# One 512-column matmul for both input parts in the four side-by-side output tiles of a mixer

## The chip, the cores and the metric

The kernel runs on one core of a Trainium2 chip. The metric is the device time of one execution in microseconds (us), as the median of several. The engines that matter are TensorE (PE in the profile; PEld is its weight loading), ScalarE (ACT), VectorE (DVE) and the DMA queues that SyncE (SP) issues. Each engine works through its own list of instructions; they wait for each other on semaphores. The schedule of TensorE, ACT and DVE is written by hand in this kernel: their instructions run in the order in which the program issues them.

## The reference

An encoder trunk of 4 layers for 256 tokens of width 1024. Each layer is a SwiGLU feed-forward block, a mixer and a second feed-forward block, each between two RMS norms and added to the stream x:

```python
for i in range(DEPTH):
    g = norm_g[i]
    x = x + 0.5 * rms_norm(swiglu(rms_norm(x, g[0]), ff1_w_in[i], ff1_w_out[i]), g[1])
    h = rms_norm(x, g[2])
    kind, j = i % N_MIXERS, i // N_MIXERS
    if kind == 0:
        m = mixer_a(h, a_w_qkv[j], a_rel_bias[j], a_w_o[j])
    elif kind == 1:
        m = mixer_b(h, b_w_in[j], b_ln_g[j], b_ln_b[j], b_w_s[j], b_b_s[j], b_w_o[j])
    else:
        m = mixer_c(h, c_w_qkv[j], c_lambda[j], c_subln_g[j], c_w_o[j], lambda_init)
    x = x + rms_norm(m, g[3])
    x = x + 0.5 * rms_norm(swiglu(rms_norm(x, g[4]), ff2_w_in[i], ff2_w_out[i]), g[5])
```

Mixer A (layers 0 and 3) is chunked attention with a relative bias, mixer B (layer 1) a gated MLP that mixes positions, mixer C (layer 2) differential attention. Each ends in the product `o @ w_o` with a 1024 x 1024 matrix, followed by the norm with gain g[3]. That output product is what the change touches.

## The kernel before

**Layout.** Activations stand transposed: the channel on the 128 partitions, the token along the row. 1024 channels are 8 blocks k of 128 input channels, or 8 tiles d of 128 output channels, each of 256 tokens (S).

**Precision.** A product in full fp32 precision is made of fp32r matmuls on split operands. A value is split into a high part (rounded to fp32r) and a low part (the rest); of the four products, high x high, high x low and low x high are summed. For an input x the parts are called h and l and lie side by side as `x[:, 0, :]` and `x[:, 1, :]`, 256 columns each. For a weight they are `wh` and `wl`.

**Weights.** `Stream` (W in the code) loads them in slices, of which a piece of 128 x 1024 is half. A piece is split by a cast on ACT (L126, `w_hi`) and a subtraction on DVE (L129, `w_lo`). `W.pump` issues the next splits, `W.settle` issues the subtraction that is still pending, `W.done` gives a piece's slot free, and `W.hold` and `W.resume` stop and restart the splitting. There are 8 slots. A piece holds all 8 blocks k of one output tile of the mixer's output product.

**Two kinds of products.** `product` (L168) issues, for each k, three matmuls of 256 columns into one accumulator of 256 columns: wh x h, wh x l and wl x h. `product2` (L182) issues two per k: wh with h and l together as 512 columns, and wl with h as 256 columns. Its accumulator has 512 columns, of which the two halves have to be added at the end. In the down product of a feed-forward block `Branch.joined` does that: ACT copies the second half from PSUM (L363), DVE adds it to the first half into the tile `yg` (L364), and `tile_done` then works from `yg`.

**The end of a tile.** `Branch.tile_done` takes a finished tile, from PSUM or from `yg`. ACT squares it (L373, for the norm's sum over channels) and scales it with the gain into `yg` (L374). DVE adds the square to the sum (L384). After tiles 4 and 5 `Ahead.tile_done` splits tiles 0 to 3 of `yg` for the next block's first product (L407 on ACT, L408 on DVE). After the last tile, TensorE sums over the partitions with a column of ones (L243), first the sum of tiles 0 to 6 and then the square of tile 7. ACT takes the root (L251), DVE the reciprocal (L253), and TensorE spreads the result over the partitions (L258). DVE then forms the update of x (L473, L479), and the next feed-forward block begins (L507). Between those steps TensorE works off a list of matmuls of that next block which can be done with the old x and the unscaled `yg` (`Ahead`, L448, 24 matmuls), so many at each place.

**The output product.** `project_out` makes tiles 0 to 3 side by side, k by k, because its inputs come in k by k as the mixer ends, and tiles 4 to 7 one after the other by `product`. For the first four the order of steps is

```python
ORDER = (0,F) (1,F) (0,T) (2,F) (1,T) (3,F) (2,T) ... (7,F) (6,T) (7,T)     # (k, low)
```

A first step (F) of a k issues wh x h and wl x h for each of the four tiles; a low step (T) issues wh x l. Ahead of the first step of each k, `between(k)` issues what the mixer still has to do: transposes of probabilities (L763), their products with the values (L885, L886 in mixer A; L1102, L1104 in C), L986 in mixer B, the transposes L1132 in C, and the splits of the result into h and l on ACT and DVE. From k = 2 on, each low step also issues the split of one weight piece.

**PSUM.** `pair()` gives one of three buffers of two banks, a bank being 512 columns of fp32. The four tiles side by side take one bank each, so two buffers; each of tiles 4 to 7 takes a buffer of its own. `bank()` gives one of two single banks for transposes, sums and spreads.

Of the kernel before, what the change touches and what calls it, by code (L numbers as in the profile page):

```python
# [18 lines left out]
S = 256  # L19
DEPTH = 4  # L20
KD = D // P
# [35 lines left out]
def encoder_trunk_kernel(  # L57
# [14 lines left out]
    nc = tc.nc  # L72
# [91 lines left out]
    def product(o, wh, wl, x, ks, at, start, stop):  # L164

        for i, k in enumerate(ks):
            for m, (w_, low) in enumerate(((wh, 0), (wh, 1), (wl, 0))):
                nc.tensor.matmul(  # L168
                    o, w_[:, at + i, :], x(k)[:, low, :], start=(start and i == 0 and m == 0),
                    stop=(stop and k == ks[-1] and m == 2),  # L170
                )
# [16 lines left out]
    def pair():  # L188
        return pp.tile([P, 2, 512], F32, tag="pp", name="pp_t")
# [208 lines left out]
    class Ahead:  # L398
# [7 lines left out]
        def parts(self, dst, src, scale):  # L406
            nc.scalar.activation(dst[:, 0, :], src, AF.Copy, scale=scale)  # L407
            nc.vector.scalar_tensor_tensor(  # L408
                dst[:, 1, :], src, scale, dst[:, 0, :].bitcast(F32), op0=ALU.mult, op1=ALU.subtract
            )  # L410
# [82 lines left out]
    def blocks(piece):  # L493
        return [part.rearrange("p (k c) -> p k c", k=KD) for part in piece]
# [144 lines left out]
    def project_out(parts, l, between, ahead):  # L639

        br = Branch(g_sb[:, l, 3, :], None, ahead)
        ws = [blocks(W.peek(e)) for e in range(4)]
        os = [ps[:, e, 0:S] for ps in (pair(), pair()) for e in range(2)]
        for k, low in ORDER:
            if not low:
                between(k)
            x = parts(k)
            for (wh, wl), o in zip(ws, os):
                for part in (wh,) if low else (wh, wl):
                    nc.tensor.matmul(  # L650
                        o, part[:, k, :], x[:, int(low), :], start=(k == 0 and part is wh and not low),
                        stop=(k == KD - 1 and low), skip_group_check=True,
                    )
            if low and k >= PUMP:
                W.pump(1)
        W.settle()
        for d in range(4):
            br.tile_done(d, os[d])
        W.done(4, 1)
        for d in range(4, KD):  # L660
            o = pair()[:, 0, 0:S]
            wh, wl = blocks(W.peek())
            product(o, wh, wl, parts, range(KD), 0, True, True)
            if d == KD - 1:
                W.hold()
                W.done()
            br.tile_done(d, o)
            if d < KD - 1:
                W.done(1, 1)
        return br.finish()  # L670
# [159 lines left out]
    def mixer_a(l, i, update):  # L830
# [86 lines left out]

        late = attention(n, softmax, transposes, v_done, mix)
        return project_out(parts, l, between, ahead)

    def mixer_b(l, i, update):
# [95 lines left out]
        def between(k):  # L1017
# [3 lines left out]
            if k == 3:  # L1021
                split(3)
                nc.scalar.preload_act_table(AF.Sqrt)

        return project_out(lambda k: op[:, k], l, between, ahead)

    def mixer_c(l, i, update):
# [144 lines left out]
        ss = small.tile([P, 16], F32, tag="sso", name="sso", bufs=1)  # L1172
        late = attention(n, softmax, transposes, v_done, mix, prepare, lambda: split(0))
        return project_out(parts, l, between, ahead)

    mixers = (mixer_a, mixer_b, mixer_c)
# [87 lines left out]
```

## Time and profile before

| | us |
|---|---|
| median of 3 runs | 1946.46 (1946.42 to 1948.36) |
| profiled execution, device time | 1947.0 |
| profiled execution, span from first to last instruction | 1945.3 |
| TensorE busy | 1931.1 |
| DVE busy | 1378.4 |
| ACT busy | 1169.6 |

The granted clock of TensorE was 0.997 of full speed over the span. The profile comes from one execution. A group's line gives the line of the program, the engine and operation, the tile written and those read, the shape and count, then the busy time and the mean duration in ns, then the idle time of the engine ahead of these instructions and what ended it. In the chain of waits each row has a start, a length and the instructions merged into it, both times in us. In a timeline a row has a start, a length, the engine and line, and in brackets how long the engine stood idle before it and for what. In a table of windows a row has the stretch, its length, the busy time and count of each engine, the granted clock, the share of the DMA engines' time, and GB/s. The durations of matmuls overlap, since they are pipelined: the time from one start to the next is shorter than one duration.

### The profile page before, as it was taken

How to read it: one execution, taken by the hardware profiler on the slowest of the kernel's cores; microseconds unless marked ns; L12 is line 12 of the kernel's file. 1: busy time of each engine (PE TensorE's matmuls, PEld its weight loads, DVE VectorE, ACT ScalarE, POOL GpSimd, SP SyncE). 2: the span in 40 equal slices, each digit the busy share in tenths (PEclk: the TensorE clock that was granted, in tenths of full speed). 3: DMA queues.
4: the chain of work that ended last, by engine and by line, in shares of the span. 5: the costliest groups of instructions: out<-in, count | busy, mean ns of one | idle time of the engine just before them, and what ended most of it. 6: DMA issues, size and time to landing. Idle time of an engine off the chain costs nothing.

```text
span 1945.3 us, 30035 instructions
## 1 busy us (share of the span) xinstructions
PE 1931.1 (99%) x12402; PEld 1745.4 (90%) x12402; DVE 1378.4 (71%) x1883; ACT 1169.6 (60%) x1805; POOL 5.2 (0%) x19
## 2 busy tenths in 40 slices
PE   9999999999999999999999999999999999999998
PEld 8888999888988889888988899988898888999887
DVE  6775867866777577877677668786767766868763
ACT  6655657656655565756565565675656555656552
POOL 0000000000000000000000000000000000000000
PEclk9999999999999999999999999999999999999999
DMA  7555524655455543655455544255545554535551
GB/s 262 205 184 202 190 108 154 232 189 184 171 196 186 205 163 141 216 195 182 165 195 195 195 155 174 109 200 196 188 155 213 180 206 161 197 123 183 203 201 44
DMA packets 50393, 350.30 MB, mean 180 GB/s; under 512 B 5712, under 2 KB 5968, under 8 KB 9040
## 3 DMA queue, kind: packets, MB, share of 16 engines
q1 hardware_dynamic: 48096, 341.86, 49.0%
q10 hardware_dynamic: 2160, 6.52, 0.9%
q8 instruction: 97, 1.59, 0.3%
q14 instruction: 40, 0.33, 0.1%
HBM read 347.31 MB, written 1.05 MB: 179 GB/s over the span
## 4 chain that ended last, share of the span: by engine, by line
PE 98%; DVE 1%; ACT 0%; DMA 0%; ACTq 0%; issue 0%; SPq 0%; DVEq 0%
PE pp_t L182 68%; PE pp_t L526 8%; PE pp_t L168 7%; PE pp_t L507 4%; PE pp_t L691 3%; PE pp_t L650 2%; PE pp_t L731 1%; PE pst_t L763 1%; PE pst_t L243 1%; PE pp_t L448 1%; PE pst_t L258 1%; PE pst_t L448 1%; PE pp_t L885 0%; PE pp_t L446 0%; DVE upd L473 0%; DMA w_raw<-in_w 0%
## 5 line engine op out<-in xcount | busy, mean ns | idle before, releaser
L129 DVE TENSOR_TENSOR w_lo<-w_raw,w_hi 128x1024 fp32r<-128x1024 f32 (+1 forms) x649 | 776.4, 1218 | 69.6 <-ACT w_hi L126 69.6
L126 ACT CAST w_hi<-w_raw 128x1024 fp32r<-128x1024 f32 (+1 forms) x649 | 668.9, 1046 | 160.1 <-PE pp_t L182 130.7
L182 PE MATMUL pp_t<-xp,w_hi 128*128 128x512 f32 x2560 | 613.7, 391 | 0.0
L182 PEld LDWEIGHTS pp_t<-xp,w_hi 128*128 128x128 f32 x2560 | 469.7, 188 | 90.4
L182 PEld LDWEIGHTS pp_t<-xp,w_lo 128*128 128x128 f32 x2560 | 329.0, 191 | 12.5
L182 PE MATMUL pp_t<-xp,w_lo 128*128 128x256 f32 x2560 | 334.6, 283 | 0.0
L597 DVE TENSOR_TENSOR gu<-pp_t,share 128x512 f32<-128x512 f32 x160 | 110.7, 692 | 206.1 <-ACT share L596 206.1
L596 ACT COPY share<-pp_t 128x512 f32<-128x512 f32 x160 | 93.6, 585 | 150.5 <-PE pp_t L182 149.5
L182 PE MATMUL pp_t<-h,w_hi 128*128 128x512 f32 x672 | 169.0, 391 | 0.0
L182 PE MATMUL pp_t<-l,w_hi 128*128 128x512 f32 x560 | 142.6, 391 | 0.0
L182 PEld LDWEIGHTS pp_t<-h,w_hi 128*128 128x128 f32 x672 | 122.1, 189 | 22.6
L567 ACT ACTIVATE gs<-gs 128x512 f32<-128x512 f32 x88 | 55.7, 633 | 141.5 <-DVE gs L566 141.5
L526 PE MATMUL pp_t<-xp,w_hi 128*128 128x256 f32 x832 | 123.8, 288 | 1.6 <-ACT xp L319 0.8
L182 PEld LDWEIGHTS pp_t<-l,w_hi 128*128 128x128 f32 x560 | 102.5, 188 | 21.1 <-DVE l L576 1.6
L526 PEld LDWEIGHTS pp_t<-xp,w_hi 128*128 128x128 f32 x832 | 111.1, 193 | 3.7 <-ACT xp L319 1.0
L364 DVE TENSOR_TENSOR yg<-pp_t,share 128x256 f32<-128x256 f32 x56 | 23.8, 425 | 108.8 <-ACT share L363 108.8
L182 PEld LDWEIGHTS pp_t<-h,w_lo 128*128 128x128 f32 x672 | 91.1, 191 | 5.0
L182 PE MATMUL pp_t<-h,w_lo 128*128 128x256 f32 x672 | 95.1, 282 | 0.0
L182 PE MATMUL pp_t<-l,w_lo 128*128 128x256 f32 x560 | 80.6, 283 | 0.0
L319 ACT ACTIVATE xp<-xr,g_sb 128x256 fp32r<-128x256 f32 x96 | 44.8, 504 | 56.4 <-DVE xr L479 54.0
L182 PEld LDWEIGHTS pp_t<-l,w_lo 128*128 128x128 f32 x560 | 75.3, 191 | 2.9
L526 PE MATMUL pp_t<-xp,w_lo 128*128 128x256 f32 x416 | 73.8, 284 | 0.0
(196 smaller groups left out, 2255.7 us busy)
## 6 DMA issues: line engine op xcount, KB each, us to landing
w_raw<-in_w SPq DMA_DIRECT2D x322, 1024.0 KB, 4.8
l<-in_a_bias ACTq DMA_DIRECT2D x8, 512.0 KB, 8.3
w_raw<-in_w SPq DMA_DIRECT2D x3, 512.0 KB, 8.5
out_y<-xr SPq DMA_DIRECT2D x4, 256.0 KB, 2.1
xr<-in_x_t SPq DMA_DIRECT2D x2, 384.0 KB, 6.7
w_raw<-in_w SPq DMA_DIRECT2D x2, 256.0 KB, 4.6
l<-in_b_ws ACTq DMA_DIRECT2D x1, 512.0 KB, 5.4
l<-in_b_ln_g ACTq DMA_DIRECT2D x1, 512.0 KB, 7.2
```

What stands on the lines that cost most here:

```text
L126: nc.scalar.copy(hi[:, cols], raw[:, cols])
L129: nc.vector.tensor_tensor(lo[:, cols], raw[:, cols], hi[:, cols].bitcast(F32), op=ALU.subtract)
L168: nc.tensor.matmul(o, w_[:, at + i, :], x(k)[:, low, :], start=(start and i == 0 and m == 0), stop=(stop and k == ks[-1] and m == 2),)
L182: nc.tensor.matmul(o[:, 0:S] if low else o, (wl if low else wh)[:, at + i, :], x(k)[:, 0, :] if low else x(k), start=(start and i == 0 and ...
L319: nc.scalar.activation(self.h[:, k, :], xr[:, k, :], AF.Copy, scale=gain[:, k:k + 1])
L448: nc.tensor.matmul(o[:, 0:S], w_, x, start=first, stop=last, skip_group_check=True)
L507: nc.tensor.matmul(o, part[:, k, :], n.x[:, k, int(low), :], start=((k, low) == JOIN[0] and i == 2 and part is ws[i][0]), stop=((k, low) = ...
L526: nc.tensor.matmul(o, part[:, k, :], n.x[:, k, low, :], start=(at == 0), stop=(at == 3 * KD - 1))
L567: nc.scalar.activation(gs, gs, AF.Silu)
L596: nc.scalar.copy(share, ps[:, :, S:2 * S])
L597: nc.vector.tensor_tensor(at.t[:, e], ps[:, :, 0:S], share, op=ALU.add)
L691: nc.tensor.matmul(self.ps[:, t, :], xs[:, kk, t * P:(t + 1) * P], ws, start=((kk, low) == self.order[0] and ws is wh and not (t == 0 and ...
```

## The change

The four tiles side by side get a whole bank of 512 columns each. The first step of a k now issues only wl x h, of 256 columns, into the first half; the low step issues wh with h and l together, of 512 columns, into the whole bank. That is two matmuls per k and tile in the place of three. The halves are added at the end by `joined`, the function that the down product uses. Tiles 4 to 7 stay as they were.

```diff
         br = Branch(g_sb[:, l, 3, :], None, ahead)
         ws = [blocks(W.peek(e)) for e in range(4)]
-        os = [ps[:, e, 0:S] for ps in (pair(), pair()) for e in range(2)]
+        os = [ps[:, e, :] for ps in (pair(), pair()) for e in range(2)]
         for k, low in ORDER:
             if not low:
                 between(k)
             x = parts(k)
             for (wh, wl), o in zip(ws, os):
-                for part in (wh,) if low else (wh, wl):
-                    nc.tensor.matmul(
-                        o, part[:, k, :], x[:, int(low), :], start=(k == 0 and part is wh and not low),
-                        stop=(k == KD - 1 and low), skip_group_check=True,
-                    )
+
+                nc.tensor.matmul(
+                    o if low else o[:, 0:S], (wh if low else wl)[:, k, :], x if low else x[:, 0, :],
+                    start=(k == 0 and not low), stop=(k == KD - 1 and low), skip_group_check=True,
+                )
             if low and k >= PUMP:
                 W.pump(1)
         W.settle()
         for d in range(4):
-            br.tile_done(d, os[d])
+            br.joined(d, os[d])
```

`joined`, which it calls now:

```python
def joined(self, d, o):
    if d == 0:
        self.yg = act.tile([P, KD, S], F32, tag="yg", name="yg")
    share = tmp.tile([P, 2, S], F32, tag="upd", name="share")[:, 0, :]
    nc.scalar.copy(share, o[:, S:2 * S])
    nc.vector.tensor_tensor(self.yg[:, d, :], o[:, 0:S], share, op=ALU.add)
    self.tile_done(d, self.yg[:, d, :])
```

## The prediction, made before the changed kernel ran

> **What bounds the kernel now.** I read the page first, then the chain that ended last in order of time, then the stretches in which the changed function runs, by windows and by timeline.
>
> ```profile
> PE 98%; DVE 1%; ACT 0%; DMA 0%; ACTq 0%; issue 0%; SPq 0%; DVEq 0%
> PE pp_t L182 68%; PE pp_t L526 8%; PE pp_t L168 7%; PE pp_t L507 4%; PE pp_t L691 3%; PE pp_t L650 2%; PE pp_t L731 1%; PE pst_t L763 1%; PE pst_t L243 1%; PE pp_t L448 1%; PE pst_t L258 1%; PE pst_t L448 1%; PE pp_t L885 0%; PE pp_t L446 0%; DVE upd L473 0%; DMA w_raw<-in_w 0%
> ```
>
> TensorE is the bound over the whole run: 98% of the chain. The changed matmul, L650, has 2% of it. ScalarE (ACT) and VectorE (DVE) hardly appear: on average they have room. But the change adds work to them in one short stage, and has to be judged there.
>
> **The price of a matmul.** In the groups by line and in the view of line L650 (times in ns) the column of durations misleads:
>
> ```profile
> L182 PE MATMUL pp_t<-xp,w_hi 128*128 128x512 f32 x2560 | 613.7, 391 | 0.0
> ```
>
> ```profile
> L650 PE MATMUL pp_t<-op,w_hi x96: 280/283/368, 291.5 to 1734.7; 128*128 128x256 f32 x96
> ```
>
> By these, three 256-column matmuls (849 ns) against one of 256 and one of 512 (674 ns) would save 175 ns. But matmuls overlap; what TensorE pays is the pitch, which the chain in order of time shows (start, length in us, instructions):
>
> ```profile
> 28.16 159.66 PE pp_t L182 x916
> ...
> 290.02 7.87 PE pp_t L650 x64
> 297.88 11.52 PE pp_t L168 x96
> ```
>
> L168 runs only 256-column matmuls: 11.52/96 = 120 ns each, three for 360 ns (L650: 7.87/64 = 123 ns, with its start). L182 alternates 512 and 256, and its 916 take 159.66 us: 174.3 ns on the mean, 348.6 ns a pair. So one k of one tile gets 11.4 ns shorter, and with 4 layers x 4 tiles x 8 k = 128 of them the change **can take out 1.46 us**, 0.37 us a layer. By the Trainium skill, "TensorE: Matmul & The Clock Gate", section "Back-to-back issue gap", a warm matmul takes N/2.4 + 2.5 ns, which makes 327.5 ns against 325.0 ns, an estimated gain of only 0.3 us in all; the trace's pitches are longer and their difference larger.
>
> **Work that moves behind waits.** In each layer the four tiles do, for each k, a first step (both weight parts with h: 8 matmuls, 0.96 us) and a low step (4, 0.48 us); steps of neighbouring k are interleaved. Afterwards the first step holds only 4 (0.48 us) and the low step four of 512 columns (4 x 228.6 ns = 0.91 us). The sum shrinks, but work slides later: where TensorE waits for something that another engine times, what slid behind the wait no longer fills it. From the timelines of layers 1, 2 and 0:
>
> ```profile
> 739.19 0.28 PE L650 MATMUL pp_t<-h,w_hi 128*128 128x256 f32 x1
> 742.60 0.58 PE L650 MATMUL pp_t<-h,w_lo 128*128 128x256 f32 x1 [3.13 <-DVE w_lo L129]
> ...
> 745.12 0.41 PE L650 MATMUL pp_t<-h,w_hi 128*128 128x256 f32 x1
> 745.33 0.41 PE L650 MATMUL pp_t<-h,w_lo 128*128 128x256 f32 x1
> ```
>
> Layer 1: seven matmuls stand ahead of the wait for the fourth piece's w_lo, later three. 0.48 us of cover goes, 0.37 us is gained: +0.1 us.
>
> ```profile
> 1227.85 1.26 ACT L1093 ACTIVATE l<-pp_t,rs 128x512 f32<-128x512 f32 x2 [0.24 <-PE pp_t L691]
> ```
>
> ```profile
> 1229.16 0.94 PE L1102 MATMUL pp_t<-l,h 128*128 128x128 f32 x6
> ...
> 1239.25 0.63 PE L1132 MATMUL pst_t<-ident,l 128*128 128x128 f32 x4
> ```
>
> Layer 2: L1102 starts as L1093 ends (1229.11), and the transposes at 1239.25 wait for a DVE chain. Behind the latter stand three first and four low steps: 4.80 us now, 3 x 0.48 + 4 x 0.914 = 5.10 us after: +0.3 us.
>
> ```profile
> 283.69 0.85 ACT L764 COPY h<-pst_t 128x384 f32<-128x384 f32 x2
> ```
>
> ```profile
> 284.57 0.82 PE L763 MATMUL pst_t<-ident,ex 128*128 128x128 f32 x6
> ```
>
> Layers 0 and 3: the second transposes (L763) need the banks which the L764 copies free at about 284.5; TensorE would come 0.5 us earlier and wait about half of that: of 0.37 us, 0.1 us stays, so -0.1 us each. Sum **+0.2 us**, between -1.5 (no wait bites) and +1.0 (all four lose as layer 2 does).
>
> **The join.** This is the large term. At the end of the four tiles each now needs ACT's copy of the second half (L363), DVE's add (L364), and only then L373 and L374, which read SBUF. The down product does precisely this already (ACT's timeline, one tile of it in layer 0):
>
> ```profile
> 474.37 0.37 ACT L363 COPY share<-pp_t 128x256 f32<-128x256 f32 x1 [2.01 <-PE pp_t L182]
> 475.23 0.42 ACT L373 ACTIVATE sq<-yg 128x256 f32<-128x256 f32 x1 [0.49 <-DVE yg L364]
> 475.68 0.51 ACT L374 ACTIVATE yg<-yg,g_sb 128x256 f32<-128x256 f32 x1
> 476.10 1.04 ACT L126 CAST w_hi<-w_raw 128x1024 fp32r<-128x1024 f32 x1
> ```
>
> ACT works in the written order and stands idle 0.49 us during the add: from copy to the next operation 1.73 us a tile. There a tile ends every 22 pairs, 7.7 us, so it is hidden. Here four end together. What ACT has to do there now, in its timeline of layer 0 and in the sums of the windows of all four layers:
>
> ```profile
> 297.68 0.38 ACT L373 ACTIVATE ysq<-pp_t 128x256 f32<-128x256 f32 x1 [1.84 <-PE pp_t L650]
> ...
> 300.18 1.10 ACT L126 CAST w_hi<-w_raw 128x1024 fp32r<-128x1024 f32 x1
> ...
> 306.56 0.38 ACT L373 ACTIVATE sq<-pp_t 128x256 f32<-128x256 f32 x1 [0.40 <-PE pp_t L168]
> ...
> 309.44 0.38 ACT L373 ACTIVATE sq<-pp_t 128x256 f32<-128x256 f32 x1 [1.20 <-PE pp_t L168]
> ```
>
> ```profile
> sum 47.04, PE 47.04 PEld 47.04 DVE 34.80 ACT 40.55 POOL 0.00; mean PE 11.76 PEld 11.76 DVE 8.70 ACT 10.14 POOL 0.00
> ```
>
> The four tiles take ACT 2.50 us (297.68 to 300.18); they will take 4 x 1.73 = 6.92 us, 4.42 us more. The row of sums covers the same stretch, from the first to the last square, in all four layers: 11.76 us each, with ACT idle 11.76 - 10.14 = 1.62 us. So that square comes 4.42 - 1.62 = 2.8 us late; less 0.2 us because the first pair of tiles ends two 512-column matmuls before the last, less 0.2 us because casts without a pause run into the next operation (0.93 us pitch at 300.18, not 1.04): **2.4 us**, between 2.3 and 2.8. Nothing covers it, since TensorE stands in front of the sums that need it (its timeline):
>
> ```profile
> 309.24 0.50 PE L243 MATMUL pst_t<-ones,ysq 128*128 128x1 f32 x4
> ...
> 309.93 0.56 PE L243 MATMUL pst_t<-ones,sq 128*128 128x1 f32 x4
> ```
>
> The second follows the square's end (309.82) at once, and everything after it (L251, L253, L258, the update) hangs on it; the 24 matmuls of the next product that fill this stretch stand mostly behind it in TensorE's queue.
>
> DVE adds a little:
>
> ```profile
> 307.32 2.35 DVE L129 TENSOR_TENSOR w_lo<-w_raw,w_hi 128x1024 fp32r<-128x1024 f32 x2
> 310.82 0.17 DVE L253 RECIPROCAL rs<-sd 128x2 f32<-128x2 f32 x1 [1.14 <-ACT sd L251]
> ```
>
> With the tiles numbered 0 to 7, the two splits stand behind tile 6's sum and end 1.15 us ahead of the reciprocal. Tile 6 is late by some 1.2 us more than tile 7 (the idle time ahead of the last square is used up only after it), and its sum also waits for a split: about +0.35 us, between 0 and 0.5. One join: 2.4 + 0.35 = **2.75 us**, four: 11.0 us.
>
> At nothing I cost: PSUM (tile 5 needs the first pair at 2.9 us, the second add frees it at 2.3; tile 6 needs the other at 5.76, just as the fourth add ends; a wait there is hidden by ACT's lateness), the four weight casts behind the join (late by as much as their users), DVE's 16 adds of 425 ns (inside ACT's waits). No DMA is added or moved, nothing on SP or POOL.
>
> **Sum:** 11.0 + 0.2 = +11.2 us. The profiled execution took 1947.0 us (span 1945.3), 0.5 above the median; 1946.5 + 11.2 = **1957.7 us**.
>
> **The rivals.**
>
> *The join is hidden.* If ACT could use its wait, only the copy's 0.37 us a tile would count, 1.5 us in all, less than the 1.62 idle. Then the full gain stays: 1946.5 - 1.5 = 1945.0 us. It decides below 0.4 us of added ACT time a tile; the down product shows 1.1. Chance 0.08, nearly all within 0.2%.
>
> *Half hidden.* ACT is late but a tile costs 1.3 to 1.5 us, with the matmul gain kept: 4 x (0.7 to 1.6) - 1.5 = +1.3 to +4.9 us, 1948 to 1951.4. It needs the add to start sooner than 0.40 us after the copy begins, which no row does. Chance 0.08.
>
> *The clock falls.* TensorE will stand idle about 2.1 us ahead of the first L243 (tile 6's sum), then half a us more. After the 3.13 us wait above, the pitch is 0.21 us, and the stage's granted clock:
>
> ```profile
> 738.40:755.60 17.20, 12.71 (x96) 12.28 (x96) 0.90 0.23 70
> ```
>
> 0.10 x 17.2 = 1.7 us lost. A wait of 1.0 us did no harm to the matmuls behind it, 228 ns each, as ever:
>
> ```profile
> PE pst_t L258 <- DVE rs L253: 1.0, 1, 1.0
> ```
>
> ```profile
> 708.38 4.57 PE pp_t L691 x20
> ```
>
>  2.1 us lies midway. If it trips: 4 x 1.2 to 1.7 more, 1962.5 to 1964.5 us. Chance 0.14. The same page, section "The HAM clock gate", has the clock halve after an idle window of about 3.4 us, and warns of gaps above 3; by that rule 2.1 us is safe, and layer 1's 3.13 agrees with it.
>
> *The durations count* and 128 x 175 ns = 22 us go: 1924 us. The chain's pitches speak against it: 0.02.
>
> The forecast itself, 1952 to 1961.5, has 0.68.
>
> **How the numbers follow.** Forecast: low end 4 x 2.3 - 1.5 = +7.7 (1954.2), high end 4 x 3.3 + 1.0 = +14.2 (1960.7), a little wider for rounding. The range 1951 to 1964 takes in most of the clock case and leaves out the hidden one. A measurement of this kernel tells 0.2% (3.9 us) from no change. Faster 0.03 (the durations, a rest of the hidden case), same 0.11 (hidden, and half of half hidden), slower 0.86.
>
> **What would show it.** L363 and L364 rise from 56 to 72; L650 has 256 matmuls, 128 of them 512 wide; TensorE issues 128 matmuls fewer. Four new waits of about 2 us ahead of L243 (on DVE's sum) and four of half a us (on ACT's square); ACT's four tiles take 6.9 us. The end of L168 to the second L243 grows from 0.7 to about 3 us. Wrong would be: ACT idle ahead of the last square, or L258 not later after the last L168 matmul. If the clock row shows under 1.00 behind the sums, the clock rival holds.

## The result and the profile after

The changed kernel took 1962.67 us in the median of 6 runs (1958.16 to 1964.52), the kernel before 1947.45 us (6 runs, 1946.42 to 1948.36). The ratio is 1.0076, with a 95% interval of 1.0065 to 1.0087: **slower by 15.2 us**. The profiled execution took 1962.17 us, its span is 1960.4 us.

The page of the changed kernel: the engines, and the chain that ended last by engine.

```profile
PE 1939.1 (99%) x12274; PEld 1743.7 (89%) x12274; DVE 1384.1 (71%) x1899; ACT 1176.7 (60%) x1821; POOL 5.3 (0%) x19
...
PE 95%; DVE 2%; ACT 2%; issue 0%; DMA 0%; SPq 0%; DVEq 0%; ACTq 0%
```

TensorE issues 128 matmuls fewer, and its share of the chain falls from 98% to 95%. DVE's share rises from 1% to 2%, ACT's from 0% to 2%. TensorE's waits (total us, times, longest us) name the place:

```profile
PE pst_t L243 <- DVE ysq L384: 6.6, 4, 1.7
PE pp_t L650 <- DVE w_lo L129: 3.6, 1, 3.6
...
PE pp_t L1102 <- ACT l L1093: 0.4, 1, 0.4
...
PE pst_t L1132 <- DVE l L1123: 0.2, 1, 0.2
```

The first row is new: once in each layer TensorE stands 1.66 us in front of the sums over the partitions. The others are waits in the mixers of layers 1 and 2, longer than before (3.1) or new, since less work stands ahead of them.

The chain in order of time gives what each layer's stage takes, from the start of the last L691 row ahead of the four tiles to the start of the next block (L507). In layer 0 the rows of the kernel before and of the changed kernel are

```profile
279.66 2.04 PE pp_t L691 x8
...
313.67 10.08 PE pp_t L507 x84
```

```profile
278.80 2.04 PE pp_t L691 x8
...
317.88 10.08 PE pp_t L507 x84
```

313.67 - 279.66 = 34.01 us before and 317.88 - 278.80 = 39.08 us after. The same difference in the same rows of each trace (in layer 1 from L168 x144, in layer 2 from the last L691 x16):

| stage, us | layer 0 | layer 1 | layer 2 | layer 3 | sum against before |
|---|---|---|---|---|---|
| before | 34.01 | 58.65 | 37.75 | 34.00 | |
| after | 39.08 | 62.70 | 40.46 | 37.94 | +15.77 |
| after, gap filled (below) | 36.50 | 61.53 | 40.45 | 36.50 | +10.57 |
| matmuls alone (below) | 33.97 | 58.82 | 37.91 | 33.97 | +0.26 |

All of the loss lies in these four stages (the span grew by 15.1 us, so the rest of it got 0.7 us shorter), and it is not the same in each: layer 2 loses 2.71 us, layer 0 loses 5.07. What the layers share is seen on ACT (timeline of layer 0, after):

```profile
296.56 0.37 ACT L363 COPY share<-pp_t 128x256 f32<-128x256 f32 x1 [1.86 <-PE pp_t L650]
297.43 0.42 ACT L373 ACTIVATE ysq<-yg 128x256 f32<-128x256 f32 x1 [0.49 <-DVE yg L364]
297.88 0.51 ACT L374 ACTIVATE yg<-yg,g_sb 128x256 f32<-128x256 f32 x1
298.29 0.35 ACT L363 COPY share<-pp_t 128x256 f32<-128x256 f32 x1
...
303.41 1.03 ACT L126 CAST w_hi<-w_raw 128x1024 fp32r<-128x1024 f32 x1
...
310.65 0.41 ACT L373 ACTIVATE sq<-pp_t 128x256 f32<-128x256 f32 x1
```

From 296.56 to 303.41 ACT spends 6.85 us on the four tiles, 0.49 us of each tile in a wait for DVE; before it was 2.50 us. No idle time is left ahead of the last square. Counted from the first L168 matmul (296.83), that square starts after 13.82 us; before, it was 309.44 less 297.72, 11.72 us. TensorE in the same stretch:

```profile
310.31 0.61 PE L243 MATMUL pst_t<-ones,ysq 128*128 128x1 f32 x4 [1.66 <-DVE ysq L384]
310.77 0.44 PE L448 MATMUL pp_t<-ahead,w_hi 128*128 128x256 f32 x1
311.01 0.42 PE L448 MATMUL pp_t<-ahead,w_lo 128*128 128x256 f32 x1
```

Behind the wait a matmul of 256 columns has a pitch of about 0.22 us, not 0.12. The windows from the wait to L507, one for each layer (stretch, length, then busy time and count of PE, PEld, DVE, ACT and POOL, then the granted clock):

```profile
308.70:317.70 9.00, 7.39 (x37) 7.39 (x38) 7.01 (x13) 4.17 (x10) 0.00 (x0) 0.62 0.62 233
771.90:779.90 8.00, 6.34 (x40) 6.08 (x40) 6.38 (x12) 4.35 (x9) 0.00 (x0) 0.79 0.64 246
1263.00:1271.50 8.50, 6.73 (x54) 6.26 (x53) 7.61 (x14) 5.60 (x13) 0.00 (x0) 1.00 0.46 173
1757.60:1765.70 8.10, 6.33 (x39) 5.85 (x38) 6.68 (x12) 4.26 (x9) 0.00 (x0) 0.79 0.71 253
```

In three of the four layers the granted clock falls behind the wait (0.62, 0.79, 0.79), in layer 2 it does not. That is the order of the layers' losses too. Windows of 0.5 us show how it falls: to 0.50, once in each of the three layers, for 6.8 us in layer 0 and for 3.4 us in layers 1 and 3. The fall begins 0.6, 1.2 and 2.1 us after the first sum has started, and so not at the wait itself. So there are two parts: a wait that all layers have, and a clock that falls in some.

### The profile page after: what moved, and what is told of

The parts are those of the page before. It is cut to its first block, busy times and chain, and to the rows that moved or that the text cites. A ratio compares the mean times of both kernels' runs of the same rounds, so it can differ in the third digit from the quotient of the medians.

```text
span 1960.4 us, 29794 instructions
## 1 busy us (share of the span) xinstructions
PE 1939.1 (99%) x12274; PEld 1743.7 (89%) x12274; DVE 1384.1 (71%) x1899; ACT 1176.7 (60%) x1821; POOL 5.3 (0%) x19
## 4 chain that ended last, share of the span: by engine, by line
PE 95%; DVE 2%; ACT 2%; issue 0%; DMA 0%; SPq 0%; DVEq 0%; ACTq 0%
PE pp_t L182 67%; PE pp_t L526 8%; PE pp_t L168 4%; PE pp_t L691 4%; PE pp_t L507 4%; PE pp_t L650 2%; PE pp_t L731 1%; DVE w_lo L129 1%; PE pst_t L763 1%; PE pst_t L258 1%; PE pst_t L243 1%; PE pst_t L448 1%; PE pp_t L448 1%; ACT yg L374 1%; PE pp_t L885 0%
## 5 line engine op out<-in xcount | busy, mean ns | idle before, releaser
L364 DVE TENSOR_TENSOR yg<-pp_t,share 128x256 f32<-128x256 f32 x72 | 30.6, 425 | 120.1 <-ACT share L363 120.1
```

## The experiments

Theory A was that of the prediction: the join, done tile by tile in ACT's written order, makes ACT late, and the matmuls themselves change next to nothing. To it was added what had been a rival there: the gap that the join opens on TensorE lets the clock fall. Each time is a median; "before" is the kernel before, measured beside it on the same chip.

### The matmuls alone

```diff
-            br.joined(d, os[d])
+            br.tile_done(d, os[d][:, 0:S])
```

> The two matmuls per k and tile as in the changed kernel, but the second halves are left out: tiles 0 to 3 are finished from the first half alone, as before the change. Theory A (the join at the four tiles' end is what costs, the matmuls change next to nothing, since what they save is lost again in waits): before +0.2 us, between -1.5 and +1.0. Rival B (the order of the matmuls, with more work behind the waits, is what costs): +8 us or more.

Measured: 1947.62 us against 1947.55, ratio 1.000 (0.999 to 1.001). Rival B is out. By the stages in the table above the matmuls cost +0.26 us in all; the prediction's term was +0.2. In layers 0 and 3 they gain 0.04 and 0.03 us of the 0.37 that the pitches allow, in layers 1 and 2 they lose 0.17 and 0.16.

### The join alone

Against the kernel before, shortened:

```diff
-        os = [ps[:, e, 0:S] for ps in (pair(), pair()) for e in range(2)]
+        os = [ps[:, e, :] for ps in (pair(), pair()) for e in range(2)]
...
-                        o, part[:, k, :], x[:, int(low), :], start=...
+                        o[:, S:2 * S] if low else o[:, 0:S], part[:, k, :], x[:, int(low), :], start=...
...
-            br.tile_done(d, os[d])
+            br.joined(d, os[d])
```

> Three matmuls of 256 columns per k and tile as before the change, but wh x l goes into the second half of the bank, and the four tiles are finished by the join of the changed kernel. Theory A: +10 to +11 us with the clock at full speed, up to +17 us in runs where the clock falls in the gap ahead of the sums. Rival B: less than +4 us.

Measured: 1963.31 us (1960.84 to 1965.48) against 1947.55, ratio 1.0083 (1.0068 to 1.0098). The join without any change to the number of matmuls costs all that the change costs, in the upper half of the range that theory A gave for it. Its four runs had granted clocks of 0.993 to 0.995.

### The changed kernel with the gap filled

```diff
-                column_sums(self.ss, self.acc, True, False)
                 self.fill = self.ahead or Warm()
                 if self.ahead:
                     self.ahead.begin()
+                    if not self.n:
+                        for _ in range(14):
+                            nc.tensor.matmul(self.ahead.ps[:, 0, 0:S], filler[:, 0:P], filler, start=True, stop=True)
+                column_sums(self.ss, self.acc, True, False)
```

> The changed kernel with 14 matmuls of 256 columns on a tile of ones, whose result is not used, ahead of the first sums behind each mixer, so that TensorE does not stand idle there. Theory A with the clock as its second part (a gap of 1.7 us ahead of the sums lets the clock fall in some layers of some runs, and that is the spread from 1958 to 1964.5 us): every run within 1 us of 1958, granted clock 0.997. Rival C (the spread comes from elsewhere, or the gap itself costs more than the clock): the same spread and a median near 1962.5 us.

Measured: 1957.99 us, five runs from 1956.99 to 1958.50, clock 0.997 to 0.998; before 1947.32, ratio 1.0057 (1.0043 to 1.0071). TensorE does more work and the kernel is 4.7 us faster than the changed one without it. Its stretch of layer 0:

```profile
309.43 1.70 PE L382 MATMUL pp_t<-filler 128*128 128x256 bf16 x14
311.25 0.61 PE L243 MATMUL pst_t<-ones,ysq 128*128 128x1 f32 x4
311.72 0.36 PE L451 MATMUL pp_t<-ahead,w_hi 128*128 128x256 f32 x1
311.92 0.28 PE L451 MATMUL pp_t<-ahead,w_lo 128*128 128x256 f32 x1
```

The 14 matmuls fill the wait, and behind it the durations are those of full speed. Rival C is out. The spread of the six runs of the changed kernel goes with the clock: with a clock of 0.997 it took 1958.16 us, 0.996: 1959.21, 0.995: 1962.17, 0.994: 1963.17, 0.993: 1964.51 and 1964.52. By the table of stages the join costs 10.57 - 0.26 = 10.3 us without the clock, 2.6 a layer, and the clock 5.2 us in the profiled execution: 2.6, 1.2, 0 and 1.4 us in layers 0 to 3.

### The join alone with the gap filled

The two edits above together.

> The join alone (three matmuls of 256 columns, halves joined tile by tile) with the same 14 idle matmuls ahead of the first sums. Theory A: the join without the clock, 1957.5 to 1958.5 us in every run, the same as the changed kernel with the filled gap; a difference between the two is what the matmuls themselves give, at most 1.5 us. Rival C: no change against the join alone (1963 us).

Measured: 1958.79 us (1957.71 to 1959.32) against 1947.39, ratio 1.0060 (1.0042 to 1.0078). Again the spread closes, and the join with three matmuls is within 1 us of the join with two. Three of its four runs lie above the 1957.5 to 1958.5 us that were expected, by up to 0.8 us.

### Two tiles joined, two not

```diff
-            br.joined(d, os[d])
+            if d < 2:
+                br.joined(d, os[d])
+            else:
+                br.tile_done(d, os[d][:, 0:S])
```

(on the join alone, with wh x l of tiles 2 and 3 in the first half)

> As the join alone, but only tiles 0 and 1 are joined; tiles 2 and 3 are finished as before. Theory A: two joins add 2.2 us to ACT, whose idle time before the last square, with its later start, is about 2.0 us: the square is hardly late, between 0 and +2 us in all. Rival D (each joined tile puts its 1.1 us on the path): half of what four tiles cost, +5 us or more.

Measured: 1948.71 us against 1947.55, ratio 1.0010 (1.0000 to 1.0019). Half of the joins cost 1.2 us and not 5: rival D is out. The first two all but fit into ACT's idle time, of which none is left ahead of the last square in this run's trace; the next two don't.

### The join in pairs

Shortened; `two` holds the two PSUM buffers:

```diff
+        sums = []
+        for ps in two:
+            share = tmp.tile([P, 2, S], F32, tag="upd", name="share")
+            nc.scalar.copy(share, ps[:, :, S:2 * S])
+            nc.vector.tensor_tensor(share, ps[:, :, 0:S], share, op=ALU.add)
+            sums.append(share)
         for d in range(4):
-            br.joined(d, os[d])
+            br.tile_done(d, sums[d // 2][:, d % 2, :])
```

> The changed kernel with another join: ACT copies the second halves of two tiles at a time, both copies ahead of all squares, DVE adds two tiles at a time, and ACT then squares and scales from that sum into yg, not in place. Theory A: ACT waits for DVE once and not four times; the four tiles take it 3.8 to 4.6 us and not 6.9, 1.3 to 2.1 more than before, which the idle time of 1.6 us and the earlier start nearly cover: before -0.5 to +3 us. Rival B: still +8 us or more, since the matmuls are those of the changed kernel.

Measured: 1948.11 us against 1947.55, ratio 1.0005 (0.9995 to 1.0014). ACT's timeline of layer 0:

```profile
297.81 1.07 ACT L661 COPY share<-pp_t 128x512 f32<-128x512 f32 x2 [1.87 <-PE pp_t L651]
299.15 0.42 ACT L373 ACTIVATE ysq<-share 128x256 f32<-128x256 f32 x1 [0.27 <-DVE share L662]
...
302.00 1.03 ACT L126 CAST w_hi<-w_raw 128x1024 fp32r<-128x1024 f32 x1
...
309.77 0.39 ACT L373 ACTIVATE sq<-pp_t 128x256 f32<-128x256 f32 x1 [0.41 <-PE pp_t L168]
```

4.19 us for the four tiles, one wait of 0.27 us for DVE, and 0.41 us of idle time ahead of the last square is still there. With this join nothing is late, and the changed matmuls end where the kernel before does. It does not beat it: there is nothing to be gained from the matmuls (above), so no version of this change was found that does.

### The copies first

Shortened by the line that makes `yg`:

```diff
+        shares = [tmp.tile([P, 2, S], F32, tag="upd", name="share") for _ in range(2)]
         for d in range(4):
-            br.joined(d, os[d])
+            nc.scalar.copy(shares[d // 2][:, d % 2, :], os[d][:, S:2 * S])
+            nc.vector.tensor_tensor(br.yg[:, d, :], os[d][:, 0:S], shares[d // 2][:, d % 2, :], op=ALU.add)
+        for d in range(4):
+            br.tile_done(d, br.yg[:, d, :])
```

> The changed kernel with the same sixteen copies and sixteen adds of one tile each, but in each layer ACT's four copies stand ahead of the four squares, so that ACT doesn't wait for DVE's add in each tile. Theory A: ACT takes 4 x 0.3 for the copies and 4 x 0.87 for squares and scalings in place, 4.7 to 4.9 us and not 6.9; the last square is late by 0.2 to 0.5 us a layer: +1 to +3 us in all. Rival E (the number of operations added to ACT and DVE is what costs, not their order): +8 us or more, as in the changed kernel.

Measured: 1956.35 us against 1947.39, ratio 1.0046 (1.0028 to 1.0064). A miss by 6 us, at +9.0 us and so where rival E had put it. But the second and fourth copy waited for DVE all the same, so that the order was only half changed: ACT took 5.74 us for the four tiles. The next run gave each copy a tile of its own:

```diff
-        shares = [tmp.tile([P, 2, S], F32, tag="upd", name="share") for _ in range(2)]
+        tags = [dict(tag="upd"), dict(tag="upd"), dict(tag="hf", bufs=3), dict(tag="hf", bufs=3)]
+        shares = [tmp.tile([P, 2, S], F32, name="share", **t)[:, 0, :] for t in tags]
```

> As the copies first, but each of the four copies goes into a tile of its own. (With two copies in one tile, the second and the fourth copy of the run before waited for DVE's add on the other half, 0.49 and 0.55 us, so that two of the four waits were left.) Theory A: ACT takes 4.5 to 4.9 us for the four tiles and not 5.7 or 6.9; the last square is late by 0 to 0.4 us a layer, +0.5 to +3 us in all. Rival E (the number of operations, which is that of the changed kernel): as the copies first, +8 us or more.

Measured: 1954.89 us against 1947.79, ratio 1.0037 (1.0023 to 1.0051). A second miss, at +7.1 us, and the reason given in the expectation fell with it. ACT's timeline of layer 0:

```profile
298.14 0.37 ACT L661 COPY share<-pp_t 128x256 f32<-128x256 f32 x1 [1.86 <-PE pp_t L650]
299.01 0.65 ACT L661 COPY share<-pp_t 128x256 f32<-128x256 f32 x2 [0.49 <-DVE yg L662]
300.20 0.37 ACT L661 COPY share<-pp_t 128x256 f32<-128x256 f32 x1 [0.55 <-DVE yg L662]
...
303.89 1.03 ACT L126 CAST w_hi<-w_raw 128x1024 fp32r<-128x1024 f32 x1
```

With the tiles numbered 0 to 3, copies 1 and 3 wait for the adds of tiles 0 and 2, though they share nothing but the PSUM buffer of two banks. So the order was changed once more:

```diff
-        for d in range(4):
+        for d in (0, 2, 1, 3):
             nc.scalar.copy(shares[d], os[d][:, S:2 * S])
```

> As the copies first with tiles of their own, but copies and adds in the order of tiles 0, 2, 1, 3, so that neighbours read different PSUM buffers. (Tiles of their own changed nothing: the second and the fourth copy still waited for the add of the tile before, which has the same PSUM buffer.) Theory A with the wait put down to the common PSUM buffer: the second copy waits no more, the third for 0.3 us at most; ACT takes 4.8 to 5.1 us for the four tiles; the last square is late by 0.3 to 0.6 us a layer, +1.5 to +4 us in all. Rival F (every second copy waits, whatever it reads): 5.7 us, +7 us. Rival E (the number of operations): +7 us.

Measured: 1950.28 us (1947.93 to 1951.51) against 1947.08, ratio 1.0018 (1.0009 to 1.0028).

```profile
296.58 1.70 ACT L661 COPY share<-pp_t 128x256 f32<-128x256 f32 x4 [1.87 <-PE pp_t L650]
298.18 0.42 ACT L373 ACTIVATE ysq<-yg 128x256 f32<-128x256 f32 x1
...
301.59 1.03 ACT L126 CAST w_hi<-w_raw 128x1024 fp32r<-128x1024 f32 x1
```

5.01 us for the four tiles and +3.2 us, as expected. (The profiled execution, 1947.93 us at a clock of 0.999, is the fastest of the ten.) In this order neighbouring copies also go to tiles of different tags in SBUF, `upd` and `hf`. That is not what took the wait away: in the join in pairs two copies into tiles of one tag, from different PSUM buffers, follow each other without a wait (297.81 above). The operations on ACT and DVE are the same 4 copies, adds, squares and scalings as in the changed kernel, which takes 15 us more than before: rivals E and F are out. It is the order.

### All of them beside each other

| kernel | ACT on the four tiles, layer 0, us | time against before, us |
|---|---|---|
| before | 2.50 | |
| matmuls alone | 2.50 | +0.1 |
| join in pairs | 4.19 | +0.6 |
| join alone, two tiles | 4.69 | +1.2 |
| copies first, crossed | 5.01 | +3.2 |
| copies first, own tiles | 5.75 | +7.1 |
| copies first | 5.74 | +9.0 |
| changed, gap filled | 6.86 | +10.7 |
| join alone, gap filled | 6.85 | +11.4 |
| changed | 6.85 | +15.2 |
| join alone | 6.86 | +15.8 |

The cost stays near nothing up to some 4.5 us: 2.50 and the 1.6 us of idle time, with the earlier start and closer casts (0.4 us). Above that each us comes back about four times, once in each layer: from the crossed copies to the changed kernel with the gap filled it is 1.85 us more of ACT and 7.5 us more in time. Where the gap is open, the clock's part is added: the copies first, with and without tiles of their own, differ by 1.9 us at the same 5.7 us of ACT, and their runs had clocks of 0.994 to 0.996.

## Why the prediction was right, and which step was off

The time fell into the range, and the sign and the mechanism of the join were those of the forecast. The forecast itself was not met: 1957.7 us was 5.0 us too low, and the measured 1962.67 us lies above its 1952 to 1961.5 us and inside the 1962.5 to 1964.5 us of the rival in which the clock falls. The range held because it took in most of that rival. Of the 5.0 us, 1.0 is the kernel before, whose median is 1947.45 us over 6 runs and was 1946.46 us over the 3 that the forecast started from. In the profiled executions the terms were: matmuls 0.2 us forecast and 0.26 measured, the join 11.0 and 10.3, the clock 0 and 5.2.

**The pitches held.** In the changed kernel four matmuls of 256 and four of 512 columns follow each other in 1.40 us, 0.35 us a pair; the gain of the durations' column (22 us) was not there.

**Work behind the waits held:** forecast -0.1, +0.1, +0.3 and -0.1 us, measured in the matmuls alone -0.04, +0.17, +0.16 and -0.03. That these waits take the gain was argued from the traces and agrees with them in size; no run took the waits away.

**The join held.** ACT per tile: forecast 1.73 us, measured 6.85/4 = 1.71. The last square late: forecast 2.4 us, measured 13.82 - 11.72 = 2.1 in layer 0, a little below the 2.3 to 2.8 allowed for. DVE's two splits ahead of the reciprocal: forecast 0.35; in layer 2, where the clock stayed up, the rows of ACT and DVE are

```profile
1268.17 0.26 ACT L251 ACTIVATE sd<-pst_t,eps_t 128x2 f32<-128x2 f32 x1 [0.33 <-PE pst_t L243]
```

```profile
1266.57 2.35 DVE L129 TENSOR_TENSOR w_lo<-w_raw,w_hi 128x1024 fp32r<-128x1024 f32 x2
1268.85 0.16 DVE L253 RECIPROCAL rs<-sd 128x2 f32<-128x2 f32 x1
```

0.68 us from the root to the reciprocal, and 0.30 before (310.52 to 310.82 in layer 0): +0.38 us. Together the join was forecast at 2.75 us a layer and measured at 2.6. Of the two waits forecast on TensorE only the first came: the list of its waits has no row for the four of half a us on ACT's square.

**The step that was off is the clock.** It stood as a rival with a chance of 0.14, because the gap "lies midway" between a wait of 1.0 us that did no harm and one of 3.1 us that did. The gap came out shorter than forecast, 1.66 us and not 2.1, and the clock fell all the same, in three of four layers of the profiled execution. The wait of 1.0 us stood in other surroundings: behind it came four spreads of 128 columns and then 512-column matmuls without a pause. Behind this one come the sums, matmuls of one column, with the spreads and matmuls of 256 columns. In the run with the copies in tiles of their own even 0.71 us ahead of the sums went with a clock of 0.73 behind it:

```profile
310.78 0.60 PE L243 MATMUL pst_t<-ones,ysq 128*128 128x1 f32 x4 [0.71 <-DVE ysq L384]
```

```profile
311.00:317.30 6.30, 6.19 (x38) 5.92 (x38) 5.18 (x10) 2.36 (x7) 0.00 (x0) 0.73 0.87 333
```

By the Trainium skill, "TensorE: Matmul & The Clock Gate", section "The HAM clock gate", the clock halves after an idle window of about 3.4 us; the gaps here are half of that and less, so as a bound on a single wait the rule does not hold in this trace, and the measurement decides. Nor did a long wait always bring the clock down: in the profiled execution of the crossed copies a wait of 3.61 us in layer 1 passed with the clock at 1.00 from ahead of it to behind it, while the 3.13 us in the kernel before went with a fall. So the length of the one wait did not decide it, and midway between two waits was no ground for a chance of 0.14. What counts in its place, the share of idle time, the thin matmuls or where a window falls, no run here separates. The price of the rival was about right: 1.2 to 1.7 us a layer forecast, 0, 1.2, 1.4 and 2.6 measured.

## What to carry to other kernels

A helper that is hidden where its calls are far apart (1.7 us every 7.7) is not hidden where four calls come at once: count its waits in the written order of the engine, against the idle time that this engine has before the next thing on the path. If halves have to be joined by two engines, put the first engine's part for all tiles ahead of the second part for any, and let neighbours read different PSUM buffers. A gap of 1.66 us on TensorE cost 1.2 to 2.6 us more in the three layers where the clock fell behind it; matmuls without a use, issued into the gap, took that cost away.

## What had not been expected of the hardware

In each layer, 14 matmuls whose result nobody reads made the changed kernel 4.7 us faster in all and closed the spread of its runs from 6.4 to 1.5 us.

The granted clock did not sink by degrees. In the changed kernel's profiled execution it went from 1.00 to 0.50 for 3.4 us, once for twice that, and up to 2.1 us after the wait had ended.

ACT's copy out of one bank waited 0.49 us for DVE's add on the other bank of the same buffer, both of them reads. The wait is a semaphore's, so it is one that the program carries. The Trainium skill, "PSUM — Partial Sum Buffer", section "PSUM bank collisions raise a hardware error", asks for such a guard between two engines on the same bank, reads included; here the two operations used different banks of one buffer and were kept apart all the same, and reading the buffers crosswise took the wait away.
